# Transposes and casts of a hybrid encoder tied behind chosen instructions, key copies reordered

## The chip, the cores and the metric

The kernel runs on one core of one Trainium2 chip. The metric is the device time of one execution in microseconds, as the median of three runs. Engines are named as the profile names them: PE is TensorE (PEld its weight loads), DVE is VectorE, ACT is ScalarE, POOL is GpSimd, SP is SyncE.

## What is computed

Two requests, of 512 and 256 tokens, go through two layers with shared weights, all in fp32. Each layer runs four heads of differential attention with ALiBi and four heads of a bidirectional mLSTM on the same input, joins them with an output projection, and follows with a convolutional gated feed-forward network. Cut to the two formulas around the change:

```python
s = jnp.einsum('bqhcd,bshcd->bhcqs', qi, k)            # two maps c per head
p = jax.nn.softmax(s + bias[None, :, None], axis=-1)
a = p[:, :, 0] - lam * p[:, :, 1]
att = _head_rmsnorm(jnp.einsum('bhqs,bshd->bqhd', a, v), att_g) * (1.0 - lam_init)
...
num = e_inter * (q @ C_prev) + ((q @ k.T) * P) @ v      # per chunk of 128, both directions
h = num / jnp.maximum(jnp.abs(den), jnp.exp(-m_out))[..., None]
...
x <- LN1(alpha*x + W_out [att ; sigmoid(lo) * rmsnorm(h)])
```

## The kernel before

The 768 tokens are six tiles of 128 rows: the 256-token request is tiles 0 and 1, the other tiles 2 to 5 (`SEQS`). A large fp32 matmul is written as three passes (`PASSES`) over a rounded part and a remainder of each operand, held as fp32r; so each product needs a cast on ScalarE (the rounded part, `hi`) and a subtraction on VectorE (the remainder, `lo`).

A layer's first part, around which the change lies, goes in five weaves (L775 to L810). `weave` draws in turn from generators, so that instructions of several chains are written down interleaved: gates beside the projections of v and of head 0, then each attention head beside the mLSTM and the gate projection `lo`, and at the end head 3 beside the splitting of the results into the operand `actB` of the output projection (`wo`, L898).

What is written down is not yet the order of the engines. A scheduler in the compiler takes the instructions as a priority list and lays out one fixed queue per engine, by its own model of durations: an instruction is placed when the model thinks its inputs ready, and among ready ones the one written earlier goes first. `prio(x)` moves a block within this list: a negative number puts it back by as many places. Each engine then works through its queue strictly in that order and waits on semaphores. Every tile has a tag; tiles of one tag share a fixed number of buffers, and a tile waits till the one whose buffer it takes has been read. PSUM's eight banks are given out so: three to `d` (projections), two to `s` (scores), one each to `t`, `u` and `L`.

The chains that the change touches:

- `att_in(h)` (L686) makes queries and keys of head h by `feat_major` (L347): 24 matmuls into `psB` (tokens 0 to 255) and 24 into `psA` (tokens 256 to 767), first for queries, then for keys. The keys go to `sK` in four ScalarE copies (L703 to L706) and to the remainder `kL` in two VectorE subtractions (L707, L708). Map 0's scores need `sK[:, 0]` (L703 and L705) and `kL[:, 0]`, map 1's the others.
- `att(h)` (L712) goes over the two sequences (for head 3 the long one first), and in each over query tiles: scores (L728, L729) into two `s` banks, VectorE's reduction to the minimum (L730), exponentials (L734), the difference of the maps (L737), transposes (L740), their copy `aT` (L742), the value matmuls (L744) into the bank `u`, and a square sum (L745). At the end of a sequence a POOL power (L750) gives the norm's factor, VectorE scales the sums into `ao` (L752, a buffer of tag `aT`, of which there are two), PE transposes them (L757) into a tile `aoT` of tag `u`, and ScalarE writes them back over `av` (L758). The transposes stand in `prio(PR_AO)`, 40 places back.
- `lstm_out(c)` (L605), for each of the six chunks: the product `kq` (L615, bank `L`), its product with the decays (L618), the scaled queries `qet` (L622), then `lstm_qk(c + 1)` (L584), which transposes query and key of the next chunk into a tile `qkT` of bank `L` (L592) and copies them to `kt` (L595, ScalarE) and `qz` (L596, L597, VectorE; one buffer). Then come the numerators of the four heads in two pairs (L633, L636; banks `L` and `t`), the denominators (L643 to L645), and the sums (L647, L648).
- `split_att(h)` (L795) casts the attention output of head h into `actB`, one cast per sequence on ScalarE (L799), and subtracts (L800; for head 0 on POOL, else on VectorE). Heads 0 to 2 are woven beside head 3, head 3 follows.

Of the kernel before, what the change touches and what calls it, by code (L numbers as in the profile page):

```python
# [3 lines left out]

# [35 lines left out]
L1 = 0  # L40
# [11 lines left out]
PR_S = -20  # L52
PR_T = -20
PR_E = 50
PR_AO = -40
PR_CONV1 = -100
PR_CONV2 = -100
SBUFS = 2
# [13 lines left out]
TAG_GT = "t"  # L72
TAG_COLT = "tL"
TAG_CU = "t"
TAG_QKT = "L"
TAG_KQ = "L"
TAG_QET = "t"
TAG_NUM = "LtLt"
TAG_AT = "tt"
TAG_AOT = "u"  # L80
TAG_LOT = "Lt"
BANKS = {"d": 3, "s": 2, "t": 1, "u": 1, "L": 1}
SEQ_ORDER = (SEQS, SEQS, SEQS, SEQS[::-1])
WO_K = (4,5,0,1,6,7,2,3)
WO_ORDER0 = (0, 1, 2, 3, 4, 5)
NSG = 3
AT1 = 11
AT2 = 8
AT3 = 12
# [116 lines left out]
def trunk(ctx, nc, tc, d, o, depth=DEPTH):  # L206
# [12 lines left out]
    @contextmanager  # L219
    def prio(offset):  # L220

        tc.cur_priority -= offset
        yield
        tc.cur_priority += offset

    def P(tag, name):
        return pp.tile([128, 512], F32, tag=tag, name=name, bufs=banks[tag])
# [117 lines left out]
                PE.matmul(ps, xh(k, t, a), (h, l)[b][:, cols], start=k + i == 0, stop=k == 7 and i == 2)  # L345

    def feat_major(blocks, psA, psB):  # L347

        for ps, tok in ((psB, slice(0, SB)), (psA, slice(SB, T))):
            n = 0  # L350
            for k in range(8):
                _, h, l = blocks[k // 4]
                for a, b in PASSES:
                    w = (h, l)[a][:, (k % 4) * 128:(k % 4 + 1) * 128]
                    PE.matmul(ps, w, actA[:, k, b, tok], start=n == 0, stop=n == 23)
                    n += 1

    def transposed_split(src, name, tag, hi, lo):

# [8 lines left out]
    for l in range(depth):  # L368
# [236 lines left out]
        def lstm_out(lc, c):  # L605
            if c == 0:
                lstm_decay(lc, c)
                lstm_qk(lc, c)
                lstm_e(lc, c)
            if c + 1 < NT:  # L610
                lstm_decay(lc, c + 1)
            pt, kt, qet, qz = pts.pop(c), kts.pop(c), qets.pop(c), kts["qz"]
            ps = P(TAG_KQ, f"kq{c}")
            for h in range(4):
                PE.matmul(ps[:, h * 128:(h + 1) * 128], kt[:, h // 2, :], qz[:, h % 2, h // 2, :], start=True, stop=True)  # L615
            for pr in range(2):
                pth = pt[:, :, 2 * pr:2 * pr + 2, :]
                V.tensor_tensor(out=pth, in0=ps[:, pr * 256:(pr + 1) * 256].rearrange("p (a b) -> p a b", a=2).unsqueeze(1).to_broadcast([128, 2, 2, 128]), in1=pth, op=ALU.mult)  # L618
            yield
            dirs = [di for di in range(2) if (di, c) in cst]  # L620
            for di in dirs:
                EN[E_QE].tensor_tensor(out=qet[:, di], in0=qz.rearrange("p h r j -> p r h j"), in1=qet[:, di], op=ALU.mult)  # L622
            if c + 1 < NT:
                lstm_qk(lc, c + 1)
            yield
            pns = {}
            for h in range(4):

                if h % 2 == 0:
                    pair = [(hh, P(TAG_NUM[hh], f"num{c}{hh}")) for hh in (h, h + 1)]  # L630
                    for hh, pn in pair:
                        for di in dirs:
                            PE.matmul(pn[:, di * 256:di * 256 + 129], qet[:, di, hh // 2, hh % 2, :], cst[di, c][:, hh // 2, :],  # L633
                                      start=di == dirs[0], stop=False, skip_group_check=True)
                        for di in range(2):
                            PE.matmul(pn[:, di * 256:di * 256 + 129], pt[:, di, hh, :], vaug[:, c, hh, :],  # L636
                                      start=not dirs and di == 0, stop=di == 1, skip_group_check=True)
                    pns.update(pair)
                    if h == 2 and c + 1 < NT:
                        lstm_e(lc, c + 1)  # L640
                pn = pns.pop(h)
                den = sm.tile([128, 2], F32, tag="den", name=f"den{c}{h}")
                V.scalar_tensor_tensor(out=den, in0=pn[:, 128::256], scalar=-1.0, in1=cols[:, c, 1, h::4], op0=ALU.mult, op1=ALU.max)  # L643
                V.tensor_tensor(out=den, in0=pn[:, 128::256], in1=den, op=ALU.max)
                V.reciprocal(den, den)  # L645
                hs = hq[:, c, h * 128:(h + 1) * 128]
                S.activation(hs, pn[:, 0:128], AF.Identity, scale=den[:, 0:1])  # L647
                V.scalar_tensor_tensor(out=hs, in0=pn[:, 256:384], scalar=den[:, 1:2], in1=hs, op0=ALU.mult, op1=ALU.add)  # L648
                S.activation(pt[:, 0, h, :], hs, AF.Square, accum_out=ssq[:, c, h:h + 1])
                if h % 2:  # L650
                    yield
            G.tensor_scalar(rsl[:, c], ssq[:, c], 128 * EPS, 1.0, op0=ALU.add, op1=ALU.mult)
            G.tensor_tensor(out=rsl[:, c], in0=rsl[:, c], in1=mhalf[:, 0:4], op=ALU.pow)
            for h in range(4):
                hs = hq[:, c, h * 128:(h + 1) * 128]
                EN[E_HS].scalar_tensor_tensor(out=hs, in0=hs, scalar=rsl[:, c, h:h + 1], in1=lstmg[:, h * 128:(h + 1) * 128], op0=ALU.mult, op1=ALU.mult)
            ready.add(c)
            gate(c)
            yield
# [23 lines left out]
            gate(t)  # L683


        def att_in(h):  # L686
            qs = 0.125 * 2.0 ** (8.0 * (h + 1) / 4)
            uq, uk = [[W.take(), W.take()] for _ in range(2)]
            pB = P("d", f"aqkB{h}")
            lo_, hi_ = slice(0, 64), slice(64, 128)  # L690
            for ui, uu in ((0, uq), (1, uk)):
                pA = P("d", f"aqkA{h}{ui}")
                pBu = pB[:, ui * 256:(ui + 1) * 256]
                feat_major(uu, pA, pBu)
                W.done(*uu)
                for ps, tk in ((pBu, slice(0, SB)), (pA, slice(SB, T))):
                    if ui == 0:
                        S.activation(sQ[lo_, 0, tk], ps[lo_], AF.Identity, scale=qs)
                        S.activation(sQ[hi_, 1, tk], ps[hi_], AF.Identity, scale=qs)
                        V.scalar_tensor_tensor(out=sQ[hi_, 0, tk], in0=ps[lo_], scalar=qs, in1=sQ[lo_, 0, tk].bitcast(F32), op0=ALU.mult, op1=ALU.subtract)  # L700
                        V.scalar_tensor_tensor(out=sQ[lo_, 1, tk], in0=ps[hi_], scalar=qs, in1=sQ[hi_, 1, tk].bitcast(F32), op0=ALU.mult, op1=ALU.subtract)
                    else:
                        S.copy(sK[lo_, 0, tk], ps[lo_])  # L703
                        S.copy(sK[hi_, 1, tk], ps[hi_])
                        S.copy(sK[hi_, 0, tk], ps[lo_])  # L705
                        S.copy(sK[lo_, 1, tk], ps[hi_])  # L706
                        V.tensor_tensor(out=kL[lo_, 0, tk], in0=ps[lo_], in1=sK[lo_, 0, tk].bitcast(F32), op=ALU.subtract)  # L707
                        V.tensor_tensor(out=kL[hi_, 1, tk], in0=ps[hi_], in1=sK[hi_, 1, tk].bitcast(F32), op=ALU.subtract)  # L708
                yield


        def att(h):  # L712
            slope = 2.0 ** (-8.0 * (h + 1) / 4)
            for s0, s1 in SEQ_ORDER[h]:
# [6 lines left out]
                for qt in range(nq):  # L721
# [19 lines left out]
                    aT = ra.tile([128, 512], F32, tag="aT", name=f"aT{h}{s0}{qt}", bufs=2)  # L741
                    CP[E_AT[qt % 2]](aT[:, :n], pa[:, :n])  # L742
                    for st in range(nq):
                        PE.matmul(pu[:, qt * 128:(qt + 1) * 128], aT[:, st * 128:(st + 1) * 128], av[:, s0 + st, h * 128:(h + 1) * 128], start=st == 0, stop=st == nq - 1)  # L744
                    S.activation(aT[:, 0:128], pu[:, qt * 128:(qt + 1) * 128], AF.Square, accum_out=ssu[:, qt:qt + 1])  # L745
                    yield

# [3 lines left out]
                ao = ra.tile([128, 512], F32, tag="aT", name=f"ao{h}{s0}", bufs=2)  # L751
                V.tensor_tensor(out=ao[:, :n].rearrange("p (a b) -> p a b", b=128), in0=pu[:, :n].rearrange("p (a b) -> p a b", b=128),  # L752
                                in1=ssu[:, :nq].unsqueeze(2).to_broadcast([128, nq, 128]), op=ALU.mult)
                pt_ = P(TAG_AOT, f"aoT{h}{s0}")
                with prio(PR_AO):
                    for qt in range(nq):
                        PE.transpose(pt_[:, qt * 128:(qt + 1) * 128], ao[:, qt * 128:(qt + 1) * 128], ident)  # L757
                S.activation(av[:, s0:s1, h * 128:(h + 1) * 128], pt_[:, :n].rearrange("p (a b) -> p a b", b=128), AF.Identity, scale=again[:, l, h:h + 1])  # L758

        def weave(*gens):  # L760

# [33 lines left out]
        def split_att(h):  # L795
            src = av[:, :, h * 128:(h + 1) * 128]
            hi, lo = (actB[:, h, i, :].rearrange("p (t q) -> p t q", t=NT) for i in range(2))
            for a, b in SEQS:
                S.copy(hi[:, a:b], src[:, a:b])  # L799
                EN[E_SPL[h]].tensor_tensor(out=lo[:, a:b], in0=src[:, a:b], in1=hi[:, a:b].bitcast(F32), op=ALU.subtract)  # L800
            yield

        def split_lstm():
            for t in range(NT):
# [5 lines left out]
                yield  # L810
            next(lo, None)

        weave((chain(att_in(3), att(3)), AT3, PR_A), (split_lstm(), 13 - L1 - L2, PR_LO), (chain(*[split_att(h) for h in range(3)]), 4))
        weave((split_att(3), 1))
        RA.close()

# [302 lines left out]
```

## Time and profile before

| | |
|---|---|
| median of 3 runs | 1814.42 us (1813.21 to 1815.66) |
| the profiled execution | 1814.85 us, its span 1813.1 us |
| PE busy / PEld busy | 1772.2 us (98%) / 1575.5 us (87%) |
| DVE / ACT / POOL busy | 1348.4 us (74%) / 774.3 us (43%) / 244.4 us (13%) |
| largest groups on PE | L942 (gate and up products) and L1002 (down products) of the feed-forward part |

The span runs from the first to the last instruction. A busy share is an average over stages. In the order of time a row gives the start, the duration of the group, the engine, the line, and in brackets the idle time before it with the instruction that ended it; rows of equal instructions in sequence are merged, with their count behind an x. Matmuls are pipelined: rows of neighbours overlap.

### The profile page before, as it was taken

Reading aid. Unit: us, or ns where it says so; the run is one execution under the profiler, and the core shown is the slowest. Engines: PE = TensorE matmul, PEld = TensorE weight load, DVE = VectorE, ACT = ScalarE, POOL = GpSimd, SP = SyncE. Lnnn points to the kernel's source line nnn. Section 1 sums busy time; section 2 is a strip of 40 time slices with the busy share of each in tenths; the row PEclk is TensorE's granted clock in tenths of the full one; section 3 lists DMA queues with packets and bytes.
Section 4 is the critical chain, followed back from the end, with each engine's and each line's share of the span. In section 5 each row is a group of like instructions: output and inputs, shape, how many; then the busy total and the mean of one; then the engine's idle time right before and its main releaser. Section 6 shows DMA issues by size and latency. Waiting matters only on the chain. (4 is left out here: it accounts for less than half of the span.)

```text
span 1813.1 us, 26263 instructions
## 1 busy us (share of the span) xinstructions
PE 1772.2 (98%) x9692; PEld 1575.5 (87%) x9692; DVE 1348.4 (74%) x2592; ACT 774.3 (43%) x1636; POOL 244.4 (13%) x266
## 2 busy tenths in 40 slices
PE   8999999999999999999999999999999999999998
PEld 8877887889889889899898778878899898898996
DVE  4546887599877787787955468876997787787778
ACT  4445667144334334344233556671453343343340
POOL 2001011141111111110110011101411110111102
PEclk9999999999999999999999999999999999999999
DMA  5312221303122122123232123122122221221211
GB/s 190 100 53 71 76 60 59 139 24 95 57 82 82 47 82 73 56 69 96 94 97 80 53 64 94 47 86 107 37 87 70 65 82 51 78 82 47 82 65 70
DMA packets 89232, 138.09 MB, mean 76 GB/s; under 512 B 7792, under 2 KB 33008, under 8 KB 89104
## 3 DMA queue, kind: packets, MB, share of 16 engines
q1 hardware_dynamic: 88384, 136.05, 23.7%
q8 instruction: 76, 1.25, 0.3%
q14 instruction: 52, 0.43, 0.1%
q10 hardware_dynamic: 720, 0.37, 0.1%
HBM read 130.00 MB, written 6.39 MB: 75 GB/s over the span
## 5 line engine op out<-in xcount | busy, mean ns | idle before, releaser
L942 PE MATMUL p<-actA,wh 128*128 128x384 f32 x1408 | 363.5, 338 | 3.2 <-DVE g L967 3.2
L171 ACT ACTIVATE wh<-raw 128x512 fp32r<-128x512 f32 (+1 forms) x348 | 215.8, 631 | 275.3 <-PE p L942 110.1
L172 DVE TENSOR_TENSOR wl<-raw,wh 128x512 fp32r<-128x512 f32 (+1 forms) x348 | 244.0, 712 | 62.2 <-ACT wh L171 61.7
L942 PE MATMUL p<-actB,wh 128*128 128x384 f32 x1056 | 270.1, 337 | 0.0
L942 PEld LDWEIGHTS p<-actA,wh 128*128 128x128 f32 x1408 | 254.7, 188 | 5.8 <-DVE g L967 3.8
L942 PE MATMUL p<-actA,wl 128*128 128x384 f32 x704 | 237.3, 337 | 0.0
L149 POOL TENSOR_TENSOR T<-raw,raw 128x512 f32<-128x512 f32 x88 | 120.3, 1370 | 837.4 <-DVE wl L172 483.9
L1002 PE MATMUL dn<-wh,actB 128*128 128x512 f32 x576 | 209.1, 396 | 1.4 <-DVE acc L1009 1.4
L171 ACT ACTIVATE wh<-T 128x512 fp32r<-128x512 f32 x176 | 108.5, 629 | 220.6 <-DVE acc L1009 105.3
L942 PEld LDWEIGHTS p<-actB,wh 128*128 128x128 f32 x1056 | 191.2, 188 | 0.0
L1002 PE MATMUL dn<-wh,ring 128*128 128x512 f32 x480 | 179.2, 397 | 1.6 <-DVE acc L1009 1.6
L942 PE MATMUL p<-actB,wl 128*128 128x384 f32 x528 | 177.2, 336 | 0.0
L1009 DVE TENSOR_TENSOR acc<-acc,dn 128x512 f32<-128x512 f32 x144 | 98.3, 683 | 72.2 <-PE dn L1002 72.0
L172 DVE TENSOR_TENSOR wl<-T,wh 128x512 fp32r<-128x512 f32 x176 | 129.8, 749 | 22.1 <-ACT wh L171 22.0
L1002 PEld LDWEIGHTS dn<-wh,actB 128*128 128x128 f32 x576 | 108.0, 188 | 30.3 <-DVE acc L1009 3.4
L942 PEld LDWEIGHTS p<-actA,wl 128*128 128x128 f32 x704 | 132.2, 188 | 0.1
L898 PE MATMUL wo<-wh,actB 128*128 128x512 f32 x384 | 122.9, 397 | 0.0
L1002 PE MATMUL dn<-wl,actB 128*128 128x512 f32 x288 | 113.2, 393 | 0.0
L1002 PEld LDWEIGHTS dn<-wh,ring 128*128 128x128 f32 x480 | 90.0, 188 | 24.6 <-DVE acc L1009 4.2
L942 PEld LDWEIGHTS p<-actB,wl 128*128 128x128 f32 x528 | 99.1, 188 | 0.0
L1002 PE MATMUL dn<-wl,ring 128*128 128x512 f32 x240 | 94.7, 395 | 0.0
L898 PEld LDWEIGHTS wo<-wh,actB 128*128 128x128 f32 x384 | 71.8, 188 | 16.2
(270 smaller groups left out, 3387.9 us busy)
## 6 DMA issues: line engine op xcount, KB each, us to landing
raw<-in_w_g_dram SPq DMA_DIRECT2D x88, 256.0 KB, 2.8
raw<-in_w_u_dram SPq DMA_DIRECT2D x88, 256.0 KB, 2.6
raw<-in_w_down_dram SPq DMA_DIRECT2D x88, 256.0 KB, 2.7
raw<-in_w_out_dram SPq DMA_DIRECT2D x32, 256.0 KB, 2.7
pt<-scr_m SPq DMA_DIRECT2D x12, 512.0 KB, 3.9
qet<-scr_e SPq DMA_DIRECT2D x12, 512.0 KB, 5.2
raw<-in_w_c_dram SPq DMA_DIRECT2D x16, 264.0 KB, 4.0
raw<-in_w_av_dram SPq DMA_DIRECT2D x16, 256.0 KB, 3.5
```

Of the source, the lines that this page charges most:

```text
L149: src["engine"].tensor_tensor(out=src["tile"], in0=a, in1=b, op=ALU.subtract)
L171: self.nc.scalar.activation(h, v, AF.Identity)
L172: self.nc.vector.tensor_tensor(out=l, in0=v, in1=h.bitcast(F32), op=ALU.subtract)
L898: PE.matmul(p, actB[:, k, a, t * 128:(t + 1) * 128], units[k][1 + b], start=n + i == 0, stop=n == 7 and i == 2)
L942: PE.matmul(ps, blk[1 + a][:, k * 128:(k + 1) * 128], x[:, k, b, :], start=k + i == 0, stop=k == 3 and i == 2)
L1002: PE.matmul(p, x, (wh_, wl_)[b], start=k + i == 0, stop=k == nf - 1 and i == 2)
L1009: V.tensor_tensor(out=z, in0=z, in1=p, op=ALU.add)
```

## The change

`TAG_QKT` and `TAG_AOT` become `s`, so both kinds of transposes go into the two banks of the scores. `tc.issue_after(ins)` gives each instruction written inside its block that runs on the engine of `ins` a place behind `ins` in that engine's queue; it adds no semaphore. It is used three times:

- The transposes of a finished sequence, with their eviction, are no longer written at the end of the sequence but kept in `pending` and written by `finish_sequence`: within a head behind the last value matmul of the next sequence's first query tile; across heads after the 48 query matmuls of the next head, tied behind the 8th of its `psA`; for the last sequence of a layer after the last weave, without a tie. `PR_AO` is gone.
- `lstm_qk(c + 1)` is written after the last pair of heads of chunk c, its transposes tied behind the last numerator matmul.
- The casts of `split_att` are tied behind head 3's last key copy; `wait_keys` holds the generator back until that copy is written.

The key copies are written in the order in which the maps use them, each with its subtraction.

```diff
-PR_AO = -40
-TAG_QKT = "L"
+TAG_QKT = "s"
-TAG_AOT = "u"
+TAG_AOT = "s"
+PIN_AO = 8
...
     def feat_major(blocks, psA, psB):
+        mid = None
...
-                    PE.matmul(ps, w, actA[:, k, b, tok], start=n == 0, stop=n == 23)
+                    mm = PE.matmul(ps, w, actA[:, k, b, tok], start=n == 0, stop=n == 23)
                     n += 1
+                    if ps is psA and n == PIN_AO:
+                        mid = mm
+        return mid
...
         def lstm_out(lc, c):
...
-            if c + 1 < NT:
-                lstm_qk(lc, c + 1)
             yield
             pns = {}
             for h in range(4):
...
-                            PE.matmul(pn[:, di * 256:di * 256 + 129], pt[:, di, hh, :], vaug[:, c, hh, :],
+                            mm = PE.matmul(pn[:, di * 256:di * 256 + 129], pt[:, di, hh, :], vaug[:, c, hh, :],
                                       start=not dirs and di == 0, stop=di == 1, skip_group_check=True)
...
                 if h % 2:
                     yield
+            if c + 1 < NT:
+                with tc.issue_after(mm.ins):
+                    lstm_qk(lc, c + 1)
             G.tensor_scalar(rsl[:, c], ssq[:, c], 128 * EPS, 1.0, op0=ALU.add, op1=ALU.mult)
...
+        last_copy = {}
+
         def att_in(h):
...
-                feat_major(uu, pA, pBu)
+                finish_sequence(feat_major(uu, pA, pBu))
...
                         S.copy(sK[lo_, 0, tk], ps[lo_])
+                        V.tensor_tensor(out=kL[lo_, 0, tk], in0=ps[lo_], in1=sK[lo_, 0, tk].bitcast(F32), op=ALU.subtract)
+                        S.copy(sK[hi_, 0, tk], ps[lo_])
                         S.copy(sK[hi_, 1, tk], ps[hi_])
-                        S.copy(sK[hi_, 0, tk], ps[lo_])
-                        S.copy(sK[lo_, 1, tk], ps[hi_])
-                        V.tensor_tensor(out=kL[lo_, 0, tk], in0=ps[lo_], in1=sK[lo_, 0, tk].bitcast(F32), op=ALU.subtract)
                         V.tensor_tensor(out=kL[hi_, 1, tk], in0=ps[hi_], in1=sK[hi_, 1, tk].bitcast(F32), op=ALU.subtract)
+                        last_copy[h] = S.copy(sK[lo_, 1, tk], ps[hi_])
                 yield
 
+        pending = []
+
+        def finish_sequence(pin):
+            while pending:
+                pending.pop(0)(pin)
 
         def att(h):
...
-                        PE.matmul(pu[:, qt * 128:(qt + 1) * 128], aT[:, st * 128:(st + 1) * 128], av[:, s0 + st, h * 128:(h + 1) * 128], start=st == 0, stop=st == nq - 1)
+                        mm = PE.matmul(pu[:, qt * 128:(qt + 1) * 128], aT[:, st * 128:(st + 1) * 128], av[:, s0 + st, h * 128:(h + 1) * 128], start=st == 0, stop=st == nq - 1)
+                    finish_sequence(mm)
...
-                pt_ = P(TAG_AOT, f"aoT{h}{s0}")
-                with prio(PR_AO):
-                    for qt in range(nq):
-                        PE.transpose(pt_[:, qt * 128:(qt + 1) * 128], ao[:, qt * 128:(qt + 1) * 128], ident)
-                S.activation(av[:, s0:s1, h * 128:(h + 1) * 128], pt_[:, :n].rearrange("p (a b) -> p a b", b=128), AF.Identity, scale=again[:, l, h:h + 1])
+
+                def finish(pin, h=h, s0=s0, s1=s1, nq=nq, n=n, ao=ao):
+                    with tc.issue_after(pin.ins) if pin is not None else nullcontext():
+                        pt_ = P(TAG_AOT, f"aoT{h}{s0}")
+                        for qt in range(nq):
+                            PE.transpose(pt_[:, qt * 128:(qt + 1) * 128], ao[:, qt * 128:(qt + 1) * 128], ident)
+                    S.activation(av[:, s0:s1, h * 128:(h + 1) * 128], pt_[:, :n].rearrange("p (a b) -> p a b", b=128), AF.Identity, scale=again[:, l, h:h + 1])
+
+                pending.append(finish)
...
         def split_att(h):
...
             for a, b in SEQS:
-                S.copy(hi[:, a:b], src[:, a:b])
+                with tc.issue_after(last_copy[3].ins):
+                    S.copy(hi[:, a:b], src[:, a:b])
                 EN[E_SPL[h]].tensor_tensor(out=lo[:, a:b], in0=src[:, a:b], in1=hi[:, a:b].bitcast(F32), op=ALU.subtract)
             yield
+
+        def wait_keys():
+            while 3 not in last_copy:
+                yield
...
-        weave((chain(att_in(3), att(3)), AT3, PR_A), (split_lstm(), 13 - L1 - L2, PR_LO), (chain(*[split_att(h) for h in range(3)]), 4))
+        weave((chain(att_in(3), att(3)), AT3, PR_A), (split_lstm(), 13 - L1 - L2, PR_LO), (chain(wait_keys(), *[split_att(h) for h in range(3)]), 4))
+        finish_sequence(None)
         weave((split_att(3), 1))
```

## Rows read from the trace of the kernel before

**Rows 1.** The page: span, TensorE's busy time, and its granted clock in 40 slices.

```profile
span 1813.1 us, 26263 instructions
...
PE 1772.2 (98%) x9692; PEld 1575.5 (87%) x9692; DVE 1348.4 (74%) x2592; ACT 774.3 (43%) x1636; POOL 244.4 (13%) x266
...
PEclk9999999999999999999999999999999999999999
```

**Rows 2.** Busy time by stretch: start:end, length, then each engine's busy time (instructions), clock, DMA.

```profile
100.00:330.00 230.00, 222.45 (x1325) 184.38 (x1324) 161.15 (x461) 139.68 (x404) 22.53 (x28) 1.00 0.25 78
...
1000.00:1232.00 232.00, 223.87 (x1330) 185.08 (x1328) 162.21 (x463) 140.05 (x405) 21.99 (x28) 1.00 0.25 79
```

**Rows 3.** Waits of TensorE over the span: total, times, longest.

```profile
PE aoT L757 <- DVE ao L752: 3.9, 6, 1.0
PE s L728 <- ACT sK L705: 3.2, 2, 1.6
...
PE qkT L592 <- DVE pt L618: 1.7, 2, 1.0
...
PE aoT L757 <- DVE cc L735: 1.6, 2, 0.8
...
PE kq L615 <- DVE hq L648: 0.6, 2, 0.3
```

**Rows 4.** TensorE in order of time, layer 0, from head 0 to head 1.

```profile
152.23 0.62 PE L355 MATMUL aqkA<-actA,wh 128*128 128x512 f32 x2
152.69 0.40 PE L355 MATMUL aqkA<-actA,wl 128*128 128x512 f32 x1
154.05 0.63 PE L757 MATMUL aoT<-ident,ao 128*128 128x128 f32 x4 [0.96 <-DVE ao L752]
```

**Rows 5.** TensorE in order of time, layer 0, end of head 3.

```profile
307.50 0.63 PE L757 MATMUL aoT<-ident,ao 128*128 128x128 f32 x4 [0.79 <-DVE cc L735]
...
309.11 0.60 PE L744 MATMUL u<-av,aT 128*128 128x128 f32 x4
...
313.72 0.40 PE L898 MATMUL wo<-wl,actB 128*128 128x512 f32 x1
314.39 0.41 PE L757 MATMUL aoT<-ident,ao 128*128 128x128 f32 x2 [0.27 <-DVE ao L752]
```

**Rows 6.** The tile aoT: its eviction, ns shortest/median/longest, first and last start.

```profile
L758 ACT ACTIVATE av<-aoT,again x16: 474/574/690, 126.1 to 1216.2; 128x256 f32<-128x256 f32 x8, 128x512 f32<-128x512 f32 x8
```

**Rows 7.** ScalarE in order of time, layer 0, around head 3's key copies.

```profile
277.73 2.58 ACT L799 CAST actB<-av 128x256 fp32r<-128x256 f32 x6
...
280.74 0.57 ACT L703 CAST sK<-aqkA 64x512 fp32r<-64x512 f32 x1
281.32 0.58 ACT L704 CAST sK<-aqkA 64x512 fp32r<-64x512 f32 x1
281.92 0.58 ACT L705 CAST sK<-aqkA 64x512 fp32r<-64x512 f32 x1
...
285.91 0.73 ACT L734 ACTIVATE tp<-tp,mn 128x512 f32<-128x512 f32 x1 [1.18 <-DVE mn L730]
```

**Rows 8.** TensorE in order of time, at the same place.

```profile
280.56 0.40 PE L345 MATMUL lo<-wh,actA 128*128 128x512 f32 x1
282.55 0.51 PE L728 MATMUL s<-sK,sQ 128*128 128x512 f32 x1 [1.59 <-ACT sK L705]
```

**Rows 9.** VectorE in order of time, at the same place.

```profile
278.99 3.08 DVE L800 TENSOR_TENSOR actB<-av,actB 128x256 fp32r<-128x256 f32 x4 [0.42 <-ACT actB L799]
```

**Rows 10.** VectorE in order of time, layer 0, chunk 3 of the mLSTM.

```profile
231.48 1.28 DVE L618 TENSOR_TENSOR pt<-kq,pt 128x512 f32<-128x512 f32 x2
```

**Rows 11.** The tile qkT: its three copies, ns shortest/median/longest.

```profile
L595 ACT COPY kt<-qkT x12: 353/373/375, 171.4 to 1148.2; 128x256 f32<-128x256 f32 x12
L596 DVE COPY qz<-qkT x12: 408/410/419, 171.9 to 1151.4; 64x256 f32<-64x256 f32 x12
L597 DVE COPY qz<-qkT x12: 427/428/429, 174.6 to 1153.9; 64x256 f32<-64x256 f32 x12
```

More of the change, by code (lines that the diff above doesn't have):

```diff
@@ L1 @@
 import math
-from contextlib import ExitStack, contextmanager
+from contextlib import ExitStack, contextmanager, nullcontext
 from itertools import islice
```

## The prediction

> **What bounds the kernel now.** I read the page first, then busy time by stretch, then the waits of TensorE, then the order of time around each long wait. On the page TensorE is busy for 98% of the span and its granted clock is full in all but the last of the 40 slices [rows 1]. The clock level of 2.4 GHz is thus not at stake: there is no slow stretch to win back, and only idle TensorE time can go. The change works in the attention and mLSTM part of each layer. There TensorE is idle for 230 - 222.45 = 7.6 us in layer 0 and 232 - 223.87 = 8.1 us in layer 1 [rows 2], 15.7 us in all, which is the ceiling of a pure gain of order. The waits name what ends that idle time [rows 3]: transposes of attention outputs (aoT) waited 3.9 + 1.6 = 5.5 us in 8 waits, the first score matmul of a head 3.2 us in two, the mLSTM transposes (qkT) 1.7 us in two. That is 10.4 us of the 15.7, and the diff touches just these three.
>
> A matmul's idle gap is not all that a stall costs. In the order of time two 512-column matmuls start at 152.23 and the next at 152.69, so one takes 0.23 us of the engine, though each row shows 0.40 us [rows 4]. The matmul at 152.69 has had its turn at 152.92, the transposes start at 154.05: 1.13 us are lost where the idle column says 0.96. So 0.17 us are to be added to each stall. The Trainium skill, Perfetto Trace Analysis, section "Tensor Engine Instruction (MATMUL, LD_WEIGHTS)", says that the end of a matmul is computed from its size, not observed; the distance of starts agrees. By the idle column alone the sum below would be 1.7 us smaller.
>
> **Transposes of attention outputs.** Sixteen groups (4 heads, 2 sequences, 2 layers) move; PE work is unchanged. Each is now tied behind the last value matmul of the next sequence's first query tile, or behind the 8th matmul of the next head's second query block. The waits come because the group stands in the queue right where the output scaling (ao, L752) was expected to be ready. At 307.50 it waited 0.79 us; the value matmul that it will follow stood at 309.11 [rows 5], 1.6 us later, so ao is ready by then. At 154.05 the group already stood behind more than 8 matmuls of that block, so the new tie alone would not move it; but it is now written down after all 48 query matmuls of that head instead of 40 places later than its own position, which gives it a later rank, and a few matmuls at 0.23 us cover 1.13 us. Three stalls of each layer go. The fourth, at 314.39, is the last group of the layer: it gets no tie, and its rank moves. It can lose its 0.27 us, or be put ahead of the ten output-projection matmuls that now cover it (10 x 0.23 = 2.3 us a layer). I take 0.5 us more for both layers, since ao's own end decides. Gain: 5.5 - 2 x 0.27 = 5.0 us, plus 6 x 0.17 = 1.0 us: **6.0 us**. The evictions (L758, 0.57 us each [rows 6]) follow later on ScalarE; their readers are the casts, which have the rest of the head as cover, and without it would come 1.6 us later. ao holds one of the two aT buffers longer; the next user is one query tile later, whose scores and exponentials hide it; without them it would cost the same 1.6 us.
>
> **Casts and key copies.** In layer 0 six casts of attention outputs (2.58 us) stand on ScalarE directly ahead of the four key copies of head 3. The score matmul needs copies L703 and L705, the first and third, which start at 280.74 and 281.92 [rows 7]. TensorE had been ready since 280.56 + 0.23 = 280.79 and started at 282.55: 1.76 us lost [rows 8]. The order of use alone brings L705 forward by one copy of 0.58 us; the tie of the casts behind the last key copy takes the other 2.58 us out. Together 3.2 us against 1.76: the stall goes in both layers, 3.2 + 2 x 0.17 = **3.5 us**. What is late next is on ScalarE: the six casts now stand between the key copies and the first exponentials, which waited 1.18 us for VectorE [rows 7]; their subtractions, 3.08 us of VectorE [rows 9], stand between the key remainders and the first score reductions, unless the planner slips them further back. So head 3's first query tile may lose 2.58 - 1.18 = 1.4 us per layer. It is hidden by gate matmuls (lo) as long as these are left; without that cover it costs 2.8 us for both layers. The subtractions of head 0 are POOL's; behind them on POOL comes only the root of the next attention norm (L750), due when the next sequence ends.
>
> **mLSTM transposes.** The four transposes, one ScalarE copy and two VectorE copies for the next chunk move from ahead of the numerator matmuls to behind the last of them, in ten of twelve chunks. No DMA goes with them; on SP they are passed by the load of the next chunk's exponentials, which does not read them, and on POOL by nothing. The stall that goes is that on L618: the transposes wanted the bank L that the product kq held until VectorE had read it, at 231.48 + 1.28 = 232.76 [rows 10], and TensorE waited till 232.91. With the bank s and the later place, 1.7 + 2 x 0.17 = **2.0 us** go. Also, the first numerator of the next pair no longer waits for the copies out of L. The new wait is the product kq of the next chunk, which cannot start until transposes (0.6 us), then L596 and L597 (0.41 + 0.43 us, the ScalarE copy of 0.37 us beside them [rows 11]) are through: about 1.45 us after the last numerator. The lower bound is nothing, since kq waits already for L648, VectorE's read of that numerator [rows 3]; the upper is 10 x 1.45 = 14.5 us, if TensorE has nothing else queued. I take the mean of the two waits on L648, 0.3 us, for each of the ten, less the 0.6 us paid now: **2.4 us**, nearer to the lower end because the row of the nearest kind is there.
>
> **Sum.** 6.0 + 3.5 + 2.0 = 11.5 us off, 2.4 + 0.5 = 2.9 us on: 8.6 us. The profiled execution took 1814.85 us (span 1813.1 and 1.75 around it), 0.4 above the median 1814.42. From the median: **1806 us**. The rest of the layer is TensorE-bound and only slides forward.
>
> **Rivals.** *New waits eat it.* VectorE serves the two qz copies behind the denominators, and kq stands early in the queue. At 0.85 us for each of ten chunks, 8.5 us, the time is 1814.4 - 11.5 + 8.5 = 1811.4 us. For it: VectorE is 70% busy there (161 of 230 us [rows 2]). Against it: kq waits today only twice. 18%.
>
> *The score banks.* Scores, aoT and qkT now share two banks. aoT holds one for 0.63 + 0.57 = 1.2 us sixteen times [rows 4, 6], qkT for 0.6 + 0.84 = 1.44 us twelve times [rows 11]: 36.5 us of hold. Whenever a score matmul is next in the queue, TensorE stands. From 32% of that hold (11.5 of 36.5) the change is a loss, at half of it, 18.3 us, the time is 1814.4 - 11.5 + 18.3 = 1821 us. Against it: today no score waits for a bank, only for key copies [rows 3]. 8%. The Trainium skill, Perfetto Trace Analysis, section "Matmuls", asks that independent groups rotate through different PSUM banks, which speaks for this rival; no run here shows the shared case.
>
> *The ties don't bind.* At the change of heads the transposes stay where they are, behind the 15th matmul or so; 2 x 1.13 = 2.3 us stay lost: 1808 us. 10%.
>
> *More goes.* The mLSTM chain is shorter and bank u is free earlier, so the planner finds better places for the rest too: all 15.7 us of idle time, 1799 us. 10%.
>
> **Numbers.** The forecast has 54%. A measurement here tells about 0.2%, 3.6 us, from no change: faster is below 1810.8, slower above 1818.0. Faster: 54 + 10 + 10 and 2 of the 18, 76%; the same 16%; slower 8%. The range from 1801 to 1813 takes in the bounds of the new waits up to the first rival and leaves out the last 8 to 10% on either side.
>
> **What would show it.** Right: waits of aoT under 1 us in all, of s on sK and of qkT on L618 gone, the casts behind the last key copy on ScalarE. Wrong: kq waiting over 5 us for qz, or s waiting for evictions of aoT or qkT, or attention stretches that are not shorter by some 4 us each.

## The result and the profile after

The changed kernel takes 1824.15 us (median of 4, 1821.84 to 1826.19) against 1814.03 us: a ratio of 1.0052, 95% interval 1.004 to 1.0064, so about 9.4 us slower. 1806 us were forecast.

From the page of the changed kernel, the lines that answer to [rows 1]:

```profile
span 1824.3 us, 26222 instructions
...
PE 1779.9 (98%) x9692; PEld 1576.6 (86%) x9692; DVE 1350.7 (74%) x2592; ACT 772.2 (42%) x1636; POOL 241.2 (13%) x266
```

This execution took 1826.19 us, the longest of the four. The clock row is as before, the span is 11.2 us longer, and TensorE counts 7.7 us more as busy for the same 9692 matmuls. So most of the loss doesn't stand in the idle column. The two stretches of [rows 2] and the waits of [rows 3]:

```profile
100.00:330.00 230.00, 220.69 (x1300) 180.07 (x1299) 159.21 (x456) 138.76 (x402) 21.08 (x28) 0.99 0.20 62
1000.00:1232.00 232.00, 221.93 (x1302) 181.43 (x1301) 160.06 (x456) 139.72 (x404) 20.36 (x27) 0.99 0.21 62
```

```profile
PE aT L753 <- DVE tp L750: 5.5, 6, 2.0
PE aoT L773 <- DVE ao L766: 2.5, 4, 0.7
PE num L635 <- DVE pt L622: 2.2, 4, 0.9
...
PE kq L619 <- DVE qz L600: 0.9, 2, 0.5
```

The waits that the change aimed at are gone or smaller: no score waits for `sK`, no `qkT` for L618 (now L622), `aoT` 2.5 us instead of 5.5. Yet TensorE is busy for 1.8 and 1.9 us less in the stretches, with 25 and 28 fewer matmuls begun: transposes `aT` and numerators now wait for VectorE.

The clock of both stretches is 0.99 where it was 1.00, which the clock row of the page is too coarse to show. In stretches of 10 us, the changed kernel first, then the kernel before (third number from the right is the clock):

```profile
310.00:320.00 10.00, 9.08 (x44) 7.66 (x45) 8.04 (x17) 7.70 (x19) 1.39 (x1) 0.83 0.31 94
1160.00:1170.00 10.00, 7.98 (x40) 6.88 (x39) 6.01 (x14) 5.67 (x17) 0.00 (x0) 0.83 0.10 29
```
```profile
310.00:320.00 10.00, 9.73 (x48) 7.56 (x47) 7.17 (x14) 6.16 (x15) 1.08 (x1) 1.00 0.67 217
1160.00:1170.00 10.00, 9.73 (x71) 8.62 (x70) 9.27 (x30) 5.63 (x18) 1.82 (x3) 1.00 0.25 72
```

From 312 to 315 us the granted clock of the changed kernel is 0.50, which is 1.2 instead of 2.4 GHz. Just before, TensorE had waited twice; the eight value matmuls that follow show 1.91 us, while eight of the same line at full clock show 1.13 us at 303.31:

```profile
310.04 0.66 PE L753 MATMUL aT<-ident,tp 128*128 128x128 f32 x4 [0.68 <-DVE actB L369]
311.58 1.54 PE L922 MATMUL wo<-wh,actB 128*128 128x512 f32 x3 [0.88 <-ACT wh L171]
312.92 1.91 PE L757 MATMUL u<-av,aT 128*128 128x128 f32 x8
```

In layer 1 the clock fell behind the wait of 2.0 us of `aT` on L750. An estimate from the rows of 10 us: 0.17 of 10 us in each layer, 3.4 of the 11.2 us by which this execution is longer. It is the smaller part: two of the four executions had a mean granted clock of 0.999, no lower than the kernel before, and took 1825.05 and 1821.84 us.

The whole loss is there when the output projection of layer 1 ends. Tile `wo` on TensorE in layers 0 and 1, before and after (durations shortest/median/longest, first and last start):

```profile
L898 PE MATMUL wo<-wh,actB x192: 388/393/485, 312.1 to 384.6; 128*128 128x512 f32 x192
L898 PE MATMUL wo<-wh,actB x192: 388/394/486, 1213.5 to 1286.0; 128*128 128x512 f32 x192
```
```profile
L922 PE MATMUL wo<-wh,actB x192: 388/394/691, 311.6 to 389.5; 128*128 128x512 f32 x192
L922 PE MATMUL wo<-wh,actB x192: 388/394/497, 1220.5 to 1297.3; 128*128 128x512 f32 x192
```

It ends 4.9 us late in layer 0 and 11.3 us late in layer 1: all of it, the half clock included. And the score matmuls of head 2 (tile `sK` on TensorE, 205 to 262 us), before and after:

```profile
L728 PE MATMUL s<-sK,sQ x12: 282/391/481, 218.1 to 254.6; 128*128 128x512 f32 x8, 128*128 128x256 f32 x4
```
```profile
L741 PE MATMUL s<-sK,sQ x10: 287/473/501, 229.3 to 261.5; 128*128 128x512 f32 x6, 128*128 128x256 f32 x4
```

They begin 11 us later, two of the twelve fall out of the window, and the median one shows 473 ns instead of 391: a matmul outside a run of its own kind shows longer than one in it. Over the span the matmuls into `s` count 2.2 us more, those into `u` 2.2 and those into `wo` 1.8: 6.2 of the 7.7 us of extra "busy" time, the matmuls at half clock among them.

ScalarE has waits that the kernel before doesn't have at all. Waits of ScalarE over the span, changed kernel:

```profile
ACT sK L715 <- DVE kL L714: 11.3, 8, 3.9
ACT sK L712 <- DVE kL L711: 4.6, 8, 0.7
```

Sixteen waits, 15.9 us: a key copy waits for the subtraction that is now written ahead of it. The longest, ScalarE and then VectorE in order of time:

```profile
218.54 0.19 ACT L651 ACTIVATION_READ_ACCUMULATOR pt<-hq 128x1 f32 x1
222.64 0.58 ACT L715 CAST sK<-aqkA 64x512 fp32r<-64x512 f32 x1 [3.91 <-DVE kL L714]
```
```profile
220.14 1.14 DVE L661 SCALAR_TENSOR_TENSOR hq<-hq,rsl,lstmg 128x128 f32<-128x128 f32 x4 [1.38 <-POOL rsl L658]
221.20 0.69 DVE L622 TENSOR_TENSOR pt<-kq,pt 128x512 f32<-128x512 f32 x1
221.91 0.69 DVE L714 TENSOR_TENSOR kL<-aqkA,sK 64x512 fp32r<-64x512 f32 x1
```

ScalarE stands from 218.73 to 222.64 behind a copy whose own input was ready, because VectorE's subtraction of the same PSUM bank stands in VectorE's queue behind work that waits for POOL. In the kernel before it is VectorE alone that waits, for the last copy, 12 times over the span. The sum of these waits, then the one at this head:

```profile
DVE kL L707 <- ACT sK L706: 12.8, 12, 2.3
```
```profile
224.77 0.68 DVE L707 TENSOR_TENSOR kL<-aqkA,sK 64x512 fp32r<-64x512 f32 x1 [0.40 <-ACT sK L706]
```

The Trainium skill, PSUM — Partial Sum Buffer, section "PSUM bank collisions raise a hardware error", says that the compiler's back end makes two instructions on different engines depend on each other if they touch the same bank and the same 32 partitions, reads included. The trace agrees for L715 (same partitions as L714). L707 here waits even for L706, which reads the other 64 partitions. The tile `sK`, which both use too, isn't the reason; in the changed kernel a copy into it and a subtraction that reads it run side by side, on two banks:

```profile
213.77 0.37 ACT L715 CAST sK<-aqkB 64x256 fp32r<-64x256 f32 x1
213.78 0.68 DVE L711 TENSOR_TENSOR kL<-aqkA,sK 64x512 fp32r<-64x512 f32 x1 [0.31 <-ACT sK L710]
```

So this program guards the whole bank.

### The profile page after: what moved, and what is told of

It is laid out like the page before. It is cut to its first block, busy times and chain, and to the rows that moved or that the text cites. A ratio compares the mean times of both kernels' runs of the same rounds, so it can differ in the third digit from the quotient of the medians.

```text
span 1824.3 us, 26222 instructions
## 1 busy us (share of the span) xinstructions
PE 1779.9 (98%) x9692; PEld 1576.6 (86%) x9692; DVE 1350.7 (74%) x2592; ACT 772.2 (42%) x1636; POOL 241.2 (13%) x266
```

## Experiments: parts of the change

Every ratio is against runs of the kernel before on the same chip; 0.001 is 1.8 us. First the change less one part, and parts of it alone.

Casts and key order only (both transposes as before):

```diff
+                with tc.issue_after(last_copy[3].ins):   # casts
+    (key copies and subtractions in the changed order)
```

> Only the tie of the casts and the key order of the change; both kinds of transposes stand as before, in their old banks. All theories: the wait of the first score matmul of head 3 (3.2 us in two) goes and nothing is added on the score banks, so 1814 - 3.5 = 1810.5 us, between 1809 and 1814 (the casts may delay the first exponentials). If this part were the cause of the loss, it would be above 1818.

Measured: 1817.5 us, 1.0017 (1.0008 to 1.0026). The part that was to give 3.5 us costs 3.1.

The changed kernel with the mLSTM transposes back in place and bank, and the one with attention output transposes back:

```diff
-TAG_QKT = "s"          (lstm_qk ahead of the numerators again)
+TAG_QKT = "L"
```

> The changed kernel with the mLSTM transposes back at their old place and in bank L; attention-output transposes still tied and in the score banks. Theory 1 (a tied group of transposes takes its turn in the two score banks long before it runs, so that the next scores are planned behind it): the attention-output groups alone still hold back the second query tile of a sequence, but the scores held back behind mLSTM transposes come free; the chain of head 3 ends some 8 us earlier than in the changed kernel and the time is about 1812 to 1817. Theory 2 (the mLSTM chain is longer because its transposes come after the last numerator): all of the loss goes, 1806 to 1810.

```diff
-TAG_AOT = "s"          (written at the end of the sequence again, PR_AO)
+TAG_AOT = "u"
```

> The changed kernel with the attention-output transposes as before (end of the sequence, 40 places back, bank u); mLSTM transposes still late and in the score banks. Theory 1: scores still start right behind an mLSTM group in the three chunks where they did, the time is between the two kernels, 1815 to 1821. Theory 2: as slow as the changed kernel or slower, 1822 to 1828, since the mLSTM chain is as long as there and the waits for ao are back.

Measured: 1816.9 us, 1.0013 (1.0004 to 1.0022), and 1816.68 us, 1.0013 (1.0004 to 1.0022). Each undoing takes about 7 us of the 9.4 back, so the parts don't add: together they cost more than apart. The clock has a share in that: the traces of these three parts show no fall of it in the two stretches.

The kernel before with nothing but both tags changed:

```diff
-TAG_QKT = "L"
+TAG_QKT = "s"
-TAG_AOT = "u"
+TAG_AOT = "s"
```

> The kernel before with only the two tags changed, both kinds of transposes in the score banks, at their old places and without ties. Theory 1, with the tie as what makes the turn long: a group here is placed as soon as its input is ready and holds a bank for 1.2 to 1.5 us, so little is lost, 1812 to 1818. If sharing the banks is enough by itself: 1822 or more. Theory 2: no loss, about 1814.

Measured: 1818.25 us, 1.0021 (1.0012 to 1.003). Sharing the two score banks costs 3.8 us without any tie, a little more than expected.

Then the ties with other banks, and without casts and key order:

```diff
-TAG_QKT = "s"
+TAG_QKT = "L"
```

> The changed kernel with one tag back: mLSTM transposes in bank L, still late and tied; attention-output transposes stay tied in the score banks. Either set of transposes alone left some 3 us of loss on top of the casts and keys (no_qk_move, no_ao), both together 10, so the loss is in their meeting. Theory 1 (both kinds take turns in the two score banks, so that the attention chain and the mLSTM chain wait for each other): with one kind out of the banks most of it goes, 1815 to 1818. Theory 2 (both are late at once, whatever the bank; VectorE and PE see the work bunched): no change, 1822 to 1826.

```diff
-TAG_AOT = "s"
+TAG_AOT = "d"
```

> The changed kernel with the attention-output transposes, still tied, in the three projection banks, mLSTM transposes tied in the score banks. Theory 1: 1815 to 1819, the scores start right behind mLSTM transposes only. Theory 2: 1822 to 1826. A loss of its own, if the projections now wait for a bank, would show as waits of lo or aqk and not of the score chain.

> All ties and places of the changed kernel, but no transposes in the score banks: mLSTM ones in L, attention ones in the projection banks. Theory 1: the scores run ahead of their exponentials again, attention ends with the gate matmuls as before, 1810 to 1816. Theory 2: still 1822 to 1826, and the scores of a query tile start as late as in the changed kernel.

(the last has both edits)

```diff
-                with tc.issue_after(last_copy[3].ins):
-    (key copies in the changed order)
+    (key copies in the old order)
```

> The changed kernel with the casts untied and the key copies in their old order; both kinds of transposes tied and in the score banks. Theory 1: the meeting of the two kinds is all that matters, 1819 to 1824, the change less the 3 us that casts and keys lost by themselves. If casts and keys are what turns the ties into a loss: 1812 to 1817.

Measured: `qkT` back in L 1818.48 us, 1.0021 (1.0011 to 1.003), 5.6 us better than the changed kernel for one letter; `aoT` in the projections' banks 1879.82 us, 1.0366 (1.035 to 1.0381); both 1854.01 us, 1.022 (1.0205 to 1.0235): both are misses. With `aoT` in `d` the last matmul of queries and keys in layer 0 starts at 302.8 us instead of 278.3, yet no projection waits for a bank in its trace; that late transpositions hold up the projections in the plan is likely, but not shown. Without casts and key order 1818.47 us, 1.0025 (1.0015 to 1.0034): these two parts cost 4.9 us inside the change.

Four parts alone, each on the kernel before:

> The kernel before with the key copies and their subtractions written in the order of use, nothing else. If the order of the key copies is what turned the 3.5 us of gain of casts_keys into 3.4 us of loss (it is made for all four heads, and brings the scores of heads 0 to 2 forward in the plan, onto reductions and transposes that are not ready): 1816 to 1819. If it is harmless: 1812 to 1815.

> The kernel before with the six casts tied behind the last key copy of head 3, nothing else. My sum: the wait of the first score of head 3 shrinks to about nothing in both layers, 3 us off, 1810 to 1812. If the casts are what lost in casts_keys (they now stand ahead of the first exponentials): 1816 to 1819.

> The kernel before with the attention-output transposes deferred, tied and in the score banks, nothing else. My sum said 6 us off, 1808. Theory 1: the second query tile of each sequence's scores now starts right behind them, and the plan loses there what the waits gave: 1812 to 1816. If the loss comes from the tie alone: 1818 or more.

> The kernel before with the mLSTM transposes late and tied, but in their old bank L. My sum said 2.0 us off and 2.4 on: 1814. Theory 1: no score is held back, 1812 to 1816. Theory 2 (late transposes lengthen the mLSTM chain, and that alone costs): 1818 or more.

| alone | median us | ratio (95%) |
|---|---|---|
| order of the key copies and subtractions | 1821.41 | 1.004 (1.0025 to 1.0055) |
| tie of the casts | 1812.16 | 0.9988 (0.9979 to 0.9998) |
| tie of `aoT`, in `s` | 1815.54 | 1.0005 (0.9995 to 1.0015) |
| late, tied `qkT`, in L | 1812.91 | 0.9996 (0.9986 to 1.0005) |

The key order is the largest loss, 7.3 us, more than the 1816 to 1819 us expected, and its trace shows the clock at 1.00 in both stretches; the tie of the casts gives 2.2 us; the others can't be told from nothing. Waits of ScalarE, then of TensorE, key order alone:

```profile
ACT sK L712 <- DVE kL L711: 10.1, 12, 2.4
...
ACT sK L715 <- DVE kL L714: 4.9, 8, 0.8
```
```profile
PE aoT L772 <- DVE ao L766: 7.4, 10, 1.0
...
PE s L741 <- ACT sK L712: 2.8, 2, 1.4
PE s L741 <- DVE mn L743: 2.7, 2, 1.4
```

The stall of [rows 8] isn't gone, though the copies are in the order of use: 2.8 us of 3.2 are left, and new waits stand beside it.

## Experiments: what in the key order costs

Two things were changed at once: the order of the copies, and the subtractions between them. Theory one lays the loss on the subtractions (ScalarE and VectorE in turn on one bank), theory two on the earlier rank of the scores.

```diff
                         S.copy(sK[lo_, 0, tk], ps[lo_])
+                        S.copy(sK[hi_, 0, tk], ps[lo_])
                         S.copy(sK[hi_, 1, tk], ps[hi_])
-                        S.copy(sK[hi_, 0, tk], ps[lo_])
                         S.copy(sK[lo_, 1, tk], ps[hi_])
                         V.tensor_tensor(out=kL[lo_, 0, tk], ...)
                         V.tensor_tensor(out=kL[hi_, 1, tk], ...)
```

> Before with the four key copies in the order of use, the two subtractions behind all four as before. Theory one, the chain: the loss of the key order comes from the subtractions written between the copies, because ScalarE and VectorE then read one PSUM bank in turn and ScalarE's next copy waits for VectorE (4.6 us in five waits of the copy on the subtraction in layer 0 where the key order stood alone). Then this one has no such wait and takes 1812 to 1816 us. Theory two, the rank: the loss comes from the earlier place that the scores get in the plan once their two copies are first; then it takes 1819 to 1822 us, as the key order alone did (1821.4).

Measured: 1813.91 us, 1.0007 (0.9999 to 1.0015), 12 runs.

```diff
                         S.copy(sK[lo_, 0, tk], ps[lo_])
+                        V.tensor_tensor(out=kL[lo_, 0, tk], ...)
                         S.copy(sK[hi_, 1, tk], ps[hi_])
+                        V.tensor_tensor(out=kL[hi_, 1, tk], ...)
                         S.copy(sK[hi_, 0, tk], ps[lo_])
                         S.copy(sK[lo_, 1, tk], ps[hi_])
-                        V.tensor_tensor(out=kL[lo_, 0, tk], ...)
-                        V.tensor_tensor(out=kL[hi_, 1, tk], ...)
```

> Before with the key copies in their old order (lo of map 0, hi of map 1, hi of map 0, lo of map 1), but each subtraction directly behind the copy that it needs. Theory one, the chain: the third copy waits for the first subtraction and the fourth for the second, 4 to 6 us of waits of ScalarE in a layer, and 1818 to 1822 us. Theory two, the rank: the scores' two copies are where they were, so 1812 to 1816 us.

Measured: 1824.51 us, 1.006 (1.0047 to 1.0073). Waits of ScalarE, then of TensorE:

```profile
ACT sK L712 <- DVE kL L711: 5.5, 12, 0.7
ACT sK L714 <- DVE kL L713: 4.9, 8, 0.8
```
```profile
PE s L741 <- ACT sK L714: 4.4, 2, 2.2
```

Theory two has fallen: the order of the copies alone costs nothing that can be told, the subtractions between them cost 10.9 us with the copies in their old order. A part of that is again the clock: in the profiled run it is 0.91 from 280 to 300 us and from 1190 to 1210, and the one run of five with a mean clock of 0.999 took 1821.83 us. L714 is here the third copy, which head 3's first score needs: TensorE's stall of [rows 8] grows from 1.6 to 2.2 us. Then the same edit on the changed kernel:

```diff
                         S.copy(sK[lo_, 0, tk], ps[lo_])
-                        V.tensor_tensor(out=kL[lo_, 0, tk], ...)
                         S.copy(sK[hi_, 0, tk], ps[lo_])
                         S.copy(sK[hi_, 1, tk], ps[hi_])
-                        V.tensor_tensor(out=kL[hi_, 1, tk], ...)
                         last_copy[h] = S.copy(sK[lo_, 1, tk], ps[hi_])
+                        V.tensor_tensor(out=kL[lo_, 0, tk], ...)
+                        V.tensor_tensor(out=kL[hi_, 1, tk], ...)
```

> The changed kernel with the two subtractions behind the four copies, which stay in the order of use. Theory one, the chain: the waits of the copies on the subtractions go (5.2 us in layer 0 of the changed kernel) and with them about the 5.6 us by which the changed kernel without casts and key order (1818.5) was better: 1816 to 1820 us. Theory two, the rank: no gain, 1822 to 1826 us.

Measured: 1817.49 us, 1.0025 (1.0015 to 1.0036). No copy waits for a subtraction in its trace, and (1.0052 - 1.0025) x 1814 = 4.9 us are back.

## Experiments: the score banks, and a better kernel

> The changed kernel with both suspected faults taken out: the subtractions behind the four key copies, and the mLSTM transposes in their old bank L (late place kept). If the two are separate causes, their gains add up (6.7 and 5.6 us): about 1812 us. If they were two ways of taking out one and the same loss: 1816 to 1818 us. What stays above the casts and late mLSTM transposes alone (1810.4) is then the price of the attention outputs in the score banks and of the order of the copies.

The edit is `TAG_QKT = "L"` on the last kernel. Measured: 1814.07 us, 1.0001 (0.9992 to 1.001): another 4.4 us. With the two edits 9.3 of the 9.4 us are gone. Alone they gave 4.9 and 5.6 us, so the gains add up but for 1.2 us, and the 1812 us expected for separate causes was 2 us too low. What the bank did is seen in the kernel with `qkT` in `s` and the subtractions last; VectorE, then TensorE, in order of time (of TensorE the rows of the tiles in `s`):

```profile
210.79 0.43 DVE L715 TENSOR_TENSOR kL<-aqkB,sK 64x256 fp32r<-64x256 f32 x1
216.06 0.42 DVE L600 COPY qz<-qkT 64x256 f32<-64x256 f32 x1 [0.20 <-ACT kt L599]
216.50 0.43 DVE L601 COPY qz<-qkT 64x256 f32<-64x256 f32 x1
```
```profile
213.55 0.60 PE L596 MATMUL qkT<-ident,hq 128*128 128x128 f32 x4
213.99 0.60 PE L773 MATMUL aoT<-ident,ao 128*128 128x128 f32 x4
228.13 0.60 PE L596 MATMUL qkT<-ident,hq 128*128 128x128 f32 x4
228.48 0.36 PE L741 MATMUL s<-sK,sQ 128*128 128x256 f32 x1
```

Head 2's first score has its keys from 211.2 us on. The tiles `qkT` and `aoT` were read out by 216.93, and no other tile of tag `s` is written from 214.6 to 228.1. Still the score starts at 228.48, right behind the next chunk's `qkT`, which is tied behind the last numerator of the chunk before. The row shows no wait in front of the score: the place is the plan's. With `qkT` in L the same score stands at 215.4, as tile `sK` on TensorE (205 to 262 us) shows for the one and the other:

```profile
L741 PE MATMUL s<-sK,sQ x9: 278/475/501, 228.5 to 261.7; 128*128 128x512 f32 x5, 128*128 128x256 f32 x4
```
```profile
L741 PE MATMUL s<-sK,sQ x12: 278/393/500, 215.4 to 254.3; 128*128 128x512 f32 x8, 128*128 128x256 f32 x4
```

That the scheduler gives out a tag's banks in the written order, so that a late tile keeps its turn while the bank is empty, is what I read from this; the rows show the order and the missing waits.

The two parts that didn't lose alone, together, and with the order of the copies:

```diff
+                with tc.issue_after(last_copy[3].ins):   # casts
+            if c + 1 < NT:                               # behind the last pair
+                with tc.issue_after(mm.ins):
+                    lstm_qk(lc, c + 1)                   # TAG_QKT = "L"
```

> The two parts that did not lose alone, together: the casts behind head 3's last key copy (alone -2.0 us) and the late mLSTM transposes in their old bank L (alone -1.2 us). If the parts add up: 1811 us. If a shift of the plan anywhere costs a few microseconds by chance, as the parts' failure to add up elsewhere suggests: 1813 to 1817 us.

> Casts behind the last key copy and late mLSTM transposes in bank L (1810.4 us together), and the four copies in the order of use with the subtractions behind them. If the order of use brings the first scores of a head forward, as the prediction had it: 1807 to 1809 us. If it is worth nothing once the casts are out of the way, as it was worth nothing alone (1813.9): 1810 to 1812 us.

Measured: 1810.44 us, 0.9983 (0.9974 to 0.9991), 3.1 us faster than before and the best kernel here; the gains of the two parts add up (2.2 + 0.7). With the copies in the order of use 1811.7 us, 0.9988 (0.9979 to 0.9997): the order gives nothing more. Busy time by stretch and the longest waits of TensorE in the best kernel:

```profile
100.00:330.00 230.00, 223.85 (x1331) 184.91 (x1330) 161.94 (x463) 138.59 (x403) 21.05 (x28) 1.00 0.24 78
1000.00:1232.00 232.00, 225.77 (x1337) 186.12 (x1336) 162.01 (x463) 137.75 (x402) 21.03 (x28) 1.00 0.24 77
```
```profile
PE aoT L773 <- DVE ao L767: 7.0, 12, 1.0
...
PE num L636 <- issue: 2.6, 4, 1.0
...
PE kq L620 <- DVE qz L602: 0.7, 2, 0.4
```

TensorE gains 1.4 and 1.9 us of busy time in the stretches, the 3.1 us of the result, although its `aoT` waits are longer (7.0 us) than before (5.5).

## Why the prediction was wrong

Four kernels above, taken in turn, add up to the loss: casts tied, late `qkT` in L and the copies in the order of use -2.2 us; with `aoT` tied in `s` 2.4 more; with `qkT` in `s` 4.4 more; with the subtractions between the copies 4.9 more: 9.5 us, where 9.4 were measured and -8.6 forecast. The last step holds what the half clock costs the changed kernel, since the trace with the subtractions last shows no fall there.

**Casts and key copies (-3.5 us).** This step failed in its sign. It said "the order of use alone brings L705 forward by one copy of 0.58 us", and priced only the order. The same hunk put VectorE's subtractions between ScalarE's copies; what that makes wait, and what is queued behind it on ScalarE, was not asked. The runs: 7.3 us lost for the hunk alone, 4.9 inside the change; the tie of the casts by itself -2.2 us, of the right sign, and the order of the copies nothing. The row for it was in the trace of before: L707 stood till the other engine had left the bank.

**The score banks (8%).** The sum left the sharing of the banks out, at nothing. The mechanism was named as a rival, with 1821 us, and is the second half of the loss: 5.6 us by the tag of `qkT` in the changed kernel, 4.4 with the subtractions last. But the sign that the prediction gave for it, "s waiting for evictions of aoT or qkT", never came: the score's late place was laid into the queue, and the hold of 36.5 us, from which its price was worked out, isn't the right measure. The 8% rested on "today no score waits for a bank", which says nothing of a bank that gets new users.

**Transposes of attention outputs (-6.0 us).** This step failed too, the largest term of the sum. The waits fell from 5.5 to 2.5 us, not under 1, and nothing came of it: alone 0.9 us slower (-0.9 to +2.7). With both faults out, what the change has more than the last kernel above is this part, at 1.0001 against 0.9988, 2.4 us with intervals that just overlap. So a sum of waits taken as a gain was wrong here: the fastest kernel has more of them, 7.0 us, than the kernel before. Whether another bank than `s` would have let this part gain, wasn't settled; in `d` it lost 66 us.

**mLSTM transposes (-2.0, new waits +2.4).** Net +0.4; measured -0.7 (-2.5 to +0.9) in bank L. Right within the error, and kq waited 0.9 us in the changed kernel, less than taken. The first rival, new waits of kq, fell with it. "The ties don't bind" and "More goes" weren't what happened. Of the signs, the waits of `s` on `sK` and of `qkT` on L618 went as for "right"; the attention stretches, not shorter by 4 us each, said "wrong".

**The clock.** "The clock level of 2.4 GHz is thus not at stake" didn't hold for the profiled execution, where it cost an estimated 3.4 us behind new waits. The rows show the order of the two, not more.

The two faults reach the output projection in different ways. Last starts on TensorE in layer 0, in us:

| kernel | gate matmuls `lo` | `aoT` | `wo` |
|---|---|---|---|
| before | 311.9 | 314.5 | 384.6 |
| key order alone | 315.5 | 316.6 | 388.2 |
| changed, subtractions last (`qkT` in `s`) | 308.7 | 325.1 | 386.8 |
| the same, `qkT` in L | 311.4 | 318.7 | 385.0 |
| changed | 307.1 | 326.7 | 389.5 |

With the key order alone the gate matmuls end 3.6 us late, and the rest with them: the gaps lie before. With `qkT` in `s` the gate matmuls, which fill TensorE, are used up 3.2 us early, and the chain of head 3 goes on for 16 us behind them, beside the output projection. That fits scores that are planned late while the filler goes ahead; how much each gap is due to which fault isn't shown.

## What to carry to other kernels

Read a reordering of evictions as a reordering on two engines: if ScalarE and VectorE both read a PSUM bank, write all copies of the one first and then the other's work, or each may wait for whatever the other has queued, as here. A tile that is made late on purpose is better kept out of rotating banks with tiles that are wanted early; the loss stood in no list of waits here, so compare the starts of the first users. Compare the granted clock in short stretches too. A wait that ends a stall is a place to look, not a gain to book: try each hunk alone.

## What was not expected of the hardware

Single runs spread more than the first three showed: 25 runs of the kernel before in one comparison lie between 1811.72 and 1817.92 us. In one case the trace shows what goes with it: the profiled run of the kernel with only the copies reordered took 1819.69 us at a median of 1813.91, and its granted clock fell in both layers, in layer 0 behind a wait of 2.23 us:

```profile
215.08 0.46 PE L638 MATMUL num<-cst,qet 128*128 128x129 f32 x2 [2.23 <-DVE qet L627]
```
```profile
210.00:220.00 10.00, 7.77 (x36) 6.45 (x35) 6.02 (x14) 2.36 (x9) 1.20 (x2) 0.83 0.33 96
1130.00:1150.00 20.00, 17.88 (x105) 15.18 (x103) 15.39 (x52) 13.14 (x44) 1.90 (x3) 0.91 0.18 52
```

In the kernel with `aoT` in `d` TensorE was busy for 203.07 of the 230 us from 100 on, and the granted clock of that stretch was 0.97:

```profile
100.00:330.00 230.00, 203.07 (x1185) 165.08 (x1183) 148.57 (x438) 127.75 (x376) 20.15 (x27) 0.97 0.17 50
```
